# Linear attention on one core: Q transposed as pairs of bf16 in 4-byte elements, and zero-padded K features for the first two pairs

## The chip, the core and the metric

The kernel runs on one core of a Trainium2 chip. A core has five engines that run side by side, each with its own instruction queue: TensorE (PE, matrix products and transposes, results in PSUM), VectorE (DVE), ScalarE (ACT), GpSimd (POOL) and SyncE (SP). In this kernel POOL and SP issue the transfers between the device memory (HBM) and the core's own memory (SBUF, 128 partitions). The transfers run on 16 DMA engines. A group of weights is loaded into PE by a separate instruction (LDWEIGHTS, shown as PEld) ahead of the matmul that uses it.

The metric is the device time of one execution in microseconds (us). Before the change the median of three runs is 126.3 us (126.06 to 126.33).

## The reference

Q, K and V have 8 batches, 12 heads, 512 rows and 64 columns each, in float32. With the features `max(0, x) + 1` of Q and K:

```python
Q_feat = np.maximum(0, Q) + 1
K_feat = np.maximum(0, K) + 1
KV = np.einsum('bhkd,bhkv->bhdv', K_feat, V)
K_sum = np.sum(K_feat, axis=2)
numerator = np.einsum('bhqd,bhdv->bhqv', Q_feat, KV)
denominator = np.einsum('bhqd,bhd->bhq', Q_feat, K_sum)
return (numerator / (denominator[:, :, :, None] + 1e-10)).astype(np.float32)
```

There are 96 heads (batch times head). Each needs a 64x64 product KV over its 512 rows, a sum over K's features, and then a product of its Q features with both, and a division by row.

## The kernel before, in words

**Tiling.** The rows of all heads are taken as one list. A *group* g is eight heads, and there are 12 groups; two groups, 2s and 2s+1, are a *pair* s, and there are six pairs. On loading, one partition holds 32 successive rows, so 16 partitions hold one head, and 128 partitions hold eight heads. Pair 0 is loaded in half loads (`load_first_q`, `load_rest_q`, `load`), the other five pairs each in one load of V, one of K and one of Q (`load_pair`), all issued by POOL and turned from float32 into bf16 on the way; only the first half of Q comes through SP, as float32, into an output buffer. For pairs 1 to 5 these loads read 2 MB of HBM each and write 1 MB of SBUF.

**K and V.** `k_features` makes K's features on DVE (line 154, through `feature`). Since the partitions hold eight heads, V must be kept apart by head: `v_blocks` writes V four times, each time multiplied by a column of a mask that is 1 on the partitions of one head in each half of the partitions and 0 elsewhere (tile `v_all`, 68 columns per block, one of them the mask itself, which yields K_sum). DVE writes blocks 0 and 1 whole and one half of block 2 (line 171), ACT the other half of block 2 and block 3 whole (line 173). `keys_values` (line 195) then multiplies 64 partitions of K's features, 64 columns as weights, with 64 partitions of V's four blocks, 272 columns. The half h of the partitions goes to PSUM tile h. In groups 0 and 1 the result is on the output partitions of that group's half, so two of these matmuls lie on different parts of the PE array; from group 2 on the output half changes with each matmul, so four do. There are 64 such matmuls per group. `keys_values_copies` (line 209) copies the sums to `kva_all` on ACT, as 64x64 blocks on a diagonal with a 65th column for K_sum, for two heads at a time.

**Q.** `q_features` (line 154 as well) makes Q's features in bf16, with two rows of 64 features beside each other, so that 128 columns go through one transpose. `transposes` (line 222) turns 128x128 pieces on PE, 16 per group, into two PSUM tiles of eight; `transpose_copies` (line 227) copies each tile to `qt` on ACT. `out_matmuls` (line 237) takes 64 columns of `qt` as weights and `kva` as the moving operand, eight matmuls to a PSUM tile; `norms` (lines 253 and 254, DVE) divides by the last column and writes the float32 output tile. Both sets of PSUM tiles have two buffers each.

**Order.** The order on each engine is that in which the code is written (`manual_schedule`). After pair 0, `iteration(s)` runs for s = 1 to 5: it forms KV for the groups of pair s and, woven in between, the output of the groups of pair s - 1. On DVE an iteration does: the four norms of group 2s-2, Q's features of both groups of the pair, K's features and V's blocks of group 2s+1, the four norms of group 2s-1, and K's features and V's blocks of the next pair's first group. On ACT: V's blocks of 2s+1, the four copies of transposes, V's blocks of 2s+2, the four KV copies. On PE: output cells of group 2s-2 with the quarters of `keys_values` for group 2s between them, the transposes of both groups, output cells and `keys_values` for group 2s+1.

**Loads and stores.** V, K and Q have two input buffers each. `load_pair(s + 2)` stands behind `iteration(s)` on POOL, so its V load waits until DVE and ACT have read the last of V of pair s (lines 111 for V and K, 124 for Q). All stores but the last two groups' go through POOL as well (line 138); the first six stand behind the last load. The stores of the last two groups go through SP, in pieces (lines 143 to 151). Until its first output, DVE's work is the mask (line 330, which waits for the identity matrix that POOL makes) and the mask columns of `v_all` (lines 338 and 339).

Of the kernel before, what the change touches and what calls it, by code (L numbers as in the profile page):

```python
# [8 lines left out]
FP32 = mybir.dt.float32  # L9
# [10 lines left out]
def kernel(  # L20
# [36 lines left out]
    o_dram = view(out, C)  # L57

    const = ctx.enter_context(tc.tile_pool(name="const", bufs=1))
    in_pool = ctx.enter_context(tc.tile_pool(name="in_pool", bufs=IN_BUFS))  # L60
    kf_pool = ctx.enter_context(tc.tile_pool(name="kf_pool", bufs=2))
    qf_pool = ctx.enter_context(tc.tile_pool(name="qf_pool", bufs=3))
    mid_pool = ctx.enter_context(tc.tile_pool(name="mid", bufs=2))
    out_pool = ctx.enter_context(tc.tile_pool(name="out_pool", bufs=OUT_BUFS))
    recip_pool = ctx.enter_context(tc.tile_pool(name="recip", bufs=4))
    psum_kva = ctx.enter_context(tc.tile_pool(name="psum_kva", bufs=2, space=bass.MemoryType.PSUM))
    psum = ctx.enter_context(tc.tile_pool(name="psum", bufs=2, space=bass.MemoryType.PSUM))
    psum_qt = ctx.enter_context(tc.tile_pool(name="psum_qt", bufs=2, space=bass.MemoryType.PSUM))

    identity = const.tile([P, P], BF16, name="identity")  # L70
    NV = 4
    v_all = const.tile([P, 2, 2, C2, 4, DV], BF16, name="v_all")

    mask_row = const.tile([P, 396], FP32, name="mask")
# [7 lines left out]
    kfs = {}  # L82
    qfs = {}
    qts = {}
    outs = {}
# [71 lines left out]

    def k_features(g):
        k_raw = raw.pop(("k", g))
        kf = kf_pool.tile([P, C2, 2, D], BF16, name="kf")  # L160
        for n in range(2):
            feature(kf[:, :, n], k_raw[:, n])
        kfs[g] = kf

    def v_blocks(g, engine):
        v_raw = raw["v", g]
        for b in range(4):
            block = v_all[:, g % 2, :, :, b, 0:D]
            cut = 2 if b < 2 else 1 if b == 2 else 0
            if engine == "dve" and cut > 0:  # L170
                nc.vector.tensor_scalar_mul(block[:, 0:cut], v_raw[:, 0:cut], mask[:, b : b + 1])  # L171
            if engine == "act" and cut < 2:
                nc.scalar.mul(out=block[:, cut:], in_=v_raw[:, cut:], mul=mask[:, b : b + 1])  # L173

    def q_features(g):
        q_raw = raw.pop(("q", g))
        qf = qf_pool.tile([P, R, C // 2, 2, D], BF16, name="qf")
        for n in range(2):
            feature(qf[:, :, :, n], q_raw[n])
        qfs[g] = qf  # L180

    def keys_values(g, lo=0, hi=C2):
        kf = kfs[g]
        if g % 2 == 0 and lo == 0:
            kva_ps[g // 2] = [psum_kva.tile([P, BANK], FP32, name="kva_ps") for _ in range(2)]
        halves = kva_ps[g // 2]
        for c in range(lo, hi):
            for n in range(2):
                if g < 2:
                    eight, first, last_c = g, (c, n) == (0, 0), (c, n) == (C2 - 1, 1)  # L190
                else:
                    eight, first, last_c = n, g % 2 == 0 and c == 0, g % 2 == 1 and c == C2 - 1
                for h in range(2):
                    ps = slice(64 * h, 64 * h + 64)
                    nc.tensor.matmul(  # L195
                        halves[h][64 * eight : 64 * eight + 64, 0 : 4 * DV],
                        lhsT=kf[ps, c, n, :],
                        rhs=v_all[ps, g % 2, n, c],
                        start=first,
                        stop=last_c,  # L200
                    )

    def keys_values_copies(s):
        halves = kva_ps[s]
        for h in range(2):
            kva = kva_diag[(2 * s + h) % NV]
            for n in range(2):
                ps = slice(64 * n, 64 * n + 64)
                nc.scalar.copy(  # L209
                    out=kva[ps, :, n, :],  # L210
                    in_=halves[h][ps, 0 : 4 * DV].rearrange("p (b x) -> p b x", b=4)[:, :, 0:D1],
                )

    def transposes(g):
        qf = qfs.pop(g)
        if g % 2 == 0:
            qts[g // 2] = mid_pool.tile([P, C, P, R], BF16, name="qt")
        qt_ps[g] = [psum_qt.tile([P, 2, R, P], BF16, name="qt_ps") for _ in range(2)]
        for half in range(2):
            for c in range(2):  # L220
                for r in range(R):
                    nc.tensor.transpose(qt_ps[g][half][:, c, r], qf[:, r, 2 * half + c, :, :], identity)  # L222

    def transpose_copies(g):
        for half, t in enumerate(qt_ps.pop(g)):
            lo = g % 2 * 4 + 2 * half
            nc.scalar.copy(out=qts[g // 2][:, lo : lo + 2], in_=t.rearrange("p c r q -> p c q r"))  # L227

    def out_matmuls(g, h, i):
        qt = qts[g // 2]  # L230
# [2 lines left out]
        for c in range(4 * i, 4 * i + 4):  # L233
            for j in range(2):
# [87 lines left out]
    with tc.manual_schedule():  # L322
# [76 lines left out]
```

## Time and profile before

| | |
|---|---|
| median of three runs | 126.3 us (126.06 to 126.33) |
| the profiled execution | 126.47 us |
| its span, first to last instruction | 124.7 us |
| PE busy | 72.2 us (58%), 1344 matmuls |
| DVE busy | 81.9 us (66%), 185 instructions |
| ACT busy | 68.4 us (55%), 73 instructions |
| POOL busy | 24.8 us (20%) |
| HBM read and written | 37.75 MB and 12.58 MB, 404 GB/s over the span |

How to read it: the page divides the span into 40 equal slices of 3.1 us, with the busy share of each engine in tenths and, for the DMA engines, the mean busy share of all 16. The *granted clock* (PEclk) is the share of TensorE's full clock that the throttle let through. A group of instructions is given as line, engine, operation, tiles and shapes, count, then busy time and mean nanoseconds of one, then the idle time of the engine just before them and what ended most of it. Instructions of one engine overlap in the records: of matmuls that follow each other the start-to-start time is shorter than the duration of one. A DMA share slightly above 1 means that packets overlapped.

### The profile page before, as it was taken

How to read it: one execution, taken by the hardware profiler on the slowest of the kernel's cores; microseconds unless marked ns; L12 is line 12 of the kernel's file. 1: busy time of each engine (PE TensorE's matmuls, PEld its weight loads, DVE VectorE, ACT ScalarE, POOL GpSimd, SP SyncE). 2: the span in 40 equal slices, each digit the busy share in tenths (PEclk: the TensorE clock that was granted, in tenths of full speed). 3: DMA queues.
4: the chain of work that ended last, by engine and by line, in shares of the span. 5: the costliest groups of instructions: out<-in, count | busy, mean ns of one | idle time of the engine just before them, and what ended most of it. 6: DMA issues, size and time to landing. Idle time of an engine off the chain costs nothing.

```text
span 124.7 us, 3086 instructions
## 1 busy us (share of the span) xinstructions
PE 72.2 (58%) x1344; PEld 54.4 (44%) x1344; DVE 81.9 (66%) x185; ACT 68.4 (55%) x73; POOL 24.8 (20%) x52
## 2 busy tenths in 40 slices
PE   0000199692397949976796927979429995550000
PEld 0000299591266725754465714567216774320000
DVE  0475643006679997999979979798997945990000
ACT  0005827928955999199947998059990196000000
POOL 6990001500000600033000890220210202000000
PEclk9999999999859995899769995599975799955555
DMA  3999999999999999999999999999999999999991
GB/s 74 344 216 217 214 212 210 214 214 222 210 212 210 218 222 212 212 212 214 221 214 213 212 216 216 218 213 210 214 350 422 413 417 413 413 413 418 411 388 64
DMA packets 8902, 32.18 MB, mean 258 GB/s; under 512 B 568, under 2 KB 824, under 8 KB 8760
## 3 DMA queue, kind: packets, MB, share of 16 engines
q0 software_dynamic: 7520, 28.84, 93.9%
q1 hardware_dynamic: 1368, 3.15, 6.8%
q8 instruction: 10, 0.16, 0.5%
q14 instruction: 4, 0.03, 0.1%
HBM read 37.75 MB, written 12.58 MB: 404 GB/s over the span
## 4 chain that ended last, share of the span: by engine, by line
PE 32%; DMA 21%; ACT 18%; DVE 14%; issue 3%; POOL 1%; ACTq 0%; POOLq 0%
PE kva_ps L195 21%; DMA k_raw<-in_K_dram 14%; ACT qt L227 9%; PE o_ps L237 7%; DMA v_raw<-in_V_dram 7%; ACT v_all L173 6%; DVE o_sb L254 6%; DVE v_all L171 4%; PE qt_ps L222 4%; ACT kva_all L209 2%; DVE kf L154 2%; DVE recip L253 1%; ACT L173 1%; POOL v_raw L111 1%; POOL k_raw L114 1%
## 5 line engine op out<-in xcount | busy, mean ns | idle before, releaser
L195 PE MATMUL kva_ps<-v_all,kf 64*64 64x272 bf16 x768 | 41.0, 330 | 19.9 <-ACT v_all L173 18.3
L195 PEld LDWEIGHTS <-kf 64*64 64x64 bf16 x768 | 28.3, 125 | 25.7 <-DVE v_all L171 16.4
L173 ACT ACTIVATE v_all<-v_raw,mask 128x1024 bf16<-128x1024 bf16 (+1 forms) x24 | 36.5, 1578 | 3.1 <-DMA v_raw<-in_V_dram 3.0
L254 DVE TENSOR_TENSOR o_sb<-o_ps,recip 128x512 f32<-128x512 f32 x48 | 33.2, 691 | 1.7
L227 ACT COPY qt<-qt_ps 128x1024 bf16<-128x1024 bf16 x24 | 22.7, 1024 | 19.6 <-PE qt_ps L222 19.6
L237 PE MATMUL o_ps<-kva_all,qt 128*64 128x130 bf16 x384 | 21.4, 253 | 14.1 <-ACT kva_all L209 9.2
L237 PEld LDWEIGHTS <-qt 128*64 128x64 bf16 x384 | 14.9, 126 | 23.8 <-issue 9.6
L171 DVE TENSOR_SCALAR v_all<-v_raw,mask 128x2048 bf16<-128x2048 bf16 (+1 forms) x36 | 22.0, 665 | 3.2 <-DMA v_raw<-in_V_dram 3.2
L154 DVE TENSOR_SCALAR kf<-k_raw 128x1024 bf16<-128x1024 bf16 x24 | 9.4, 434 | 12.0 <-DMA k_raw<-in_K_dram 12.0
L222 PE MATMUL qt_ps<-identity,qf 128*128 128x128 bf16 x192 | 13.7, 219 | 4.9 <-ACT qt L227 4.8
L253 DVE RECIPROCAL recip<-o_ps 128x8 f32<-128x8 f32 x48 | 9.6, 201 | 8.3 <-PE o_ps L237 8.2
L111 POOL DMA_DIRECT2D v_raw<-in_V_dram x5 | 3.7, 730 | 53.5 <-ACT qt L227 23.7
L222 PEld LDWEIGHTS <-qf 128*128 128x128 bf16 x192 | 11.2, 97 | 7.0 <-issue 6.4
L138 POOL DMA_DIRECT2D out_dram<-o_sb x10 | 8.1, 819 | 25.5 <-DVE o_sb L254 13.7
L209 ACT CAST kva_all<-kva_ps 64x260 bf16<-64x260 f32 x24 | 9.0, 374 | 3.8 <-PE kva_ps L195 3.5
L154 DVE TENSOR_SCALAR qf<-q_raw 128x1024 bf16<-128x1024 bf16 x22 | 8.2, 430 | 0.1
L173 ACT ACT_TABLE_LOAD x1 | 1.3, 1283 | 10.7 <-DMA v_raw<-in_V_dram 10.7
L124 POOL DMA_DIRECT2D q_raw<-in_Q_dram x5 | 3.6, 722 | 0.0
L111 POOL DMA_DIRECT2D k_raw<-in_K_dram x5 | 3.6, 719 | 0.0
L330 DVE TENSOR_REDUCE mask<-identity 128x4 f32<-128x128 bf16 x1 | 0.3, 285 | 4.7 <-POOL identity masks.py:199 4.7
L344 POOL MEMSET kva_all<- 128x130 bf16 x16 | 2.4, 204 | 0.0
L339 DVE CAST v_all<-mask 128x128 bf16<-128x128 f32 x2 | 2.2, 1644 | 0.0
(11 smaller groups left out, 6.0 us busy)
## 6 DMA issues: line engine op xcount, KB each, us to landing
out_dram<-o_sb POOLq DMA_DIRECT2D x10, 1024.0 KB, 24.6
v_raw<-in_V_dram POOLq DMA_DIRECT2D x5, 1024.0 KB, 13.5
k_raw<-in_K_dram POOLq DMA_DIRECT2D x5, 1024.0 KB, 17.7
q_raw<-in_Q_dram POOLq DMA_DIRECT2D x5, 1024.0 KB, 21.9
o_sb<-in_Q_dram SPq DMA_DIRECT2D x1, 1024.0 KB, 5.0
k_raw<-in_K_dram POOLq DMA_DIRECT2D x2, 512.0 KB, 9.7
v_raw<-in_V_dram POOLq DMA_DIRECT2D x2, 512.0 KB, 11.6
out_dram<-o_sb SPq DMA_DIRECT2D x1, 1024.0 KB, 11.5
```

Of the source, the lines that this page charges most:

```text
L111: nc.gpsimd.dma_start(out=t, in_=drams[x][:, 2 * s : 2 * s + 2])
L138: nc.gpsimd.dma_start(out=o_to[:, g % 2 : 2 * NP : 2], in_=outs[s][:, g % 2 : 2 * NP : 2], single_packet=True)
L154: nc.vector.tensor_scalar(out=dst, in0=src, scalar1=1.0, scalar2=1.0, op0=ALU.add, op1=ALU.max)
L171: nc.vector.tensor_scalar_mul(block[:, 0:cut], v_raw[:, 0:cut], mask[:, b : b + 1])
L173: nc.scalar.mul(out=block[:, cut:], in_=v_raw[:, cut:], mul=mask[:, b : b + 1])
L195: nc.tensor.matmul(halves[h][64 * eight : 64 * eight + 64, 0 : 4 * DV], lhsT=kf[ps, c, n, :], rhs=v_all[ps, g % 2, n, c], start=first, sto ...
L209: nc.scalar.copy(out=kva[ps, :, n, :], in_=halves[h][ps, 0 : 4 * DV].rearrange("p (b x) -> p b x", b=4)[:, :, 0:D1],)
L222: nc.tensor.transpose(qt_ps[g][half][:, c, r], qf[:, r, 2 * half + c, :, :], identity)
L227: nc.scalar.copy(out=qts[g // 2][:, lo : lo + 2], in_=t.rearrange("p c r q -> p c q r"))
L237: nc.tensor.matmul(o_ps[64 * j : 64 * j + 64, c // 2 % 2, (c % 2) * W : (c % 2) * W + W], lhsT=qt[:, c, q : q + 16, :], rhs=kva[:, b], sta ...
L253: nc.vector.reciprocal(out=recip, in_=cells[:, :, :, :, D:D1])
L254: nc.vector.tensor_tensor(out=outs[g // 2][:, 2 * h + g % 2 : 2 * NP : NP, 4 * i : 4 * i + 4].rearrange("p n (b c) d -> p b c n d", b=2), ...
```

## The change

The change has five parts.

1. Q's features are written so that the elements of two rows alternate (`qf` gets a last dimension of 2). Two bf16 are then taken as one 4-byte element (`bitcast(FP32)`) and turned with a float32 identity: eight transposes of 128x128 4-byte elements per group in place of sixteen of bf16. The copies to `qt` move 512 4-byte elements per partition in place of 1024 bf16. `out_matmuls` reads every second bf16 of `qt` as weights. `qf` has two buffers in place of three.
2. For groups 0 to 3 (`WIDE = 2` pairs), K's features of the lower and the upper 64 partitions go to different columns of a tile twice as wide, whose other columns are zero on those partitions. One matmul then takes all 128 partitions and 128 weight columns: 32 matmuls per group in place of 64. `keys_values_copies` reads the sums from where they now lie. Groups 4 to 11 keep the four-part form.
3. The tiles for K's features are no longer taken from a pool in turn, but are two fixed ones; their zero columns are set at the start, by four instructions on DVE.
4. Block 2 of V is written wholly by ACT; DVE's half of it is gone.
5. The mask's row is 48 elements in place of 396, and `recip_pool` stands earlier.

```diff
-    qf_pool = ctx.enter_context(tc.tile_pool(name="qf_pool", bufs=3))
+    qf_pool = ctx.enter_context(tc.tile_pool(name="qf_pool", bufs=2))
...
-    identity = const.tile([P, P], BF16, name="identity")
+    identity = const.tile([P, P], FP32, name="identity")
...
+    WIDE = 2
+    kf_all = [wide.tile([P, C2, 2, 2, D], BF16, name=f"kf_all_{i}") for i in range(2)]
...
     def k_features(g):
         k_raw = raw.pop(("k", g))
-        kf = kf_pool.tile([P, C2, 2, D], BF16, name="kf")
+        kf = kf_all[g % 2]
         for n in range(2):
-            feature(kf[:, :, n], k_raw[:, n])
-        kfs[g] = kf
+            if g // 2 < WIDE:
+                for h in range(2):
+                    ps = slice(64 * h, 64 * h + 64)
+                    feature(kf[ps, :, n, h], k_raw[ps, n])
+            else:
+                feature(kf[:, :, n, 0], k_raw[:, n])
...
-            cut = 2 if b < 2 else 1 if b == 2 else 0
+            cut = 2 if b < 2 else 0
...
-        qf = qf_pool.tile([P, R, C // 2, 2, D], BF16, name="qf")
+        qf = qf_pool.tile([P, R, C // 4, 2, D, 2], BF16, name="qf")
         for n in range(2):
-            feature(qf[:, :, :, n], q_raw[n])
+            feature(
+                qf[:, :, :, n].rearrange("p r c d x -> p r c x d"),
+                q_raw[n].rearrange("p r (c x) d -> p r c x d", x=2),
+            )
...
+                if g // 2 < WIDE:
+                    nc.tensor.matmul(
+                        halves[eight][:, 0 : 4 * DV],
+                        lhsT=kf[:, c, n],
+                        rhs=v_all[:, g % 2, n, c],
+                        start=first,
+                        stop=last_c,
+                    )
+                    continue
...
     def transposes(g):
-        qf = qfs.pop(g)
+        qf = qfs.pop(g).rearrange("p r c n d x -> p r c (n d x)").bitcast(FP32)
         if g % 2 == 0:
-            qts[g // 2] = mid_pool.tile([P, C, P, R], BF16, name="qt")
-        qt_ps[g] = [psum_qt.tile([P, 2, R, P], BF16, name="qt_ps") for _ in range(2)]
+            qts[g // 2] = mid_pool.tile([P, C // 2, P, R, 2], BF16, name="qt")
+        qt_ps[g] = [psum_qt.tile([P, R, P], FP32, name="qt_ps") for _ in range(2)]
         for half in range(2):
-            for c in range(2):
-                for r in range(R):
-                    nc.tensor.transpose(qt_ps[g][half][:, c, r], qf[:, r, 2 * half + c, :, :], identity)
+            for r in range(R):
+                nc.tensor.transpose(qt_ps[g][half][:, r], qf[:, r, half], identity)
 
     def transpose_copies(g):
+        to = qts[g // 2].rearrange("p c q r x -> p c (q r x)").bitcast(FP32)
         for half, t in enumerate(qt_ps.pop(g)):
-            lo = g % 2 * 4 + 2 * half
-            nc.scalar.copy(out=qts[g // 2][:, lo : lo + 2], in_=t.rearrange("p c r q -> p c q r"))
+            nc.scalar.copy(
+                out=to[:, g % 2 * 2 + half].rearrange("p (q r) -> p q r", r=R),
+                in_=t.rearrange("p r q -> p q r"),
+            )
...
-                    lhsT=qt[:, c, q : q + 16, :],
+                    lhsT=qt[:, c // 2, q : q + 16, :, c % 2],
...
+        for t in kf_all:
+            for h in range(2):
+                zeros = t[64 - 64 * h : P - 64 * h].rearrange("p c n h d -> p (c n) h d")[:, :, h]
+                nc.vector.memset(zeros.bitcast(FP32), 0.0)
```

In the built program each of the 4-byte transposes is one instruction on PE, without a separate load of weights; all other matmuls keep theirs. The order of the work on each engine is otherwise that of before.

More of the change, by code (lines that the diff above doesn't have):

```diff
@@ L59 @@
     const = ctx.enter_context(tc.tile_pool(name="const", bufs=1))
+    recip_pool = ctx.enter_context(tc.tile_pool(name="recip", bufs=4))
+    wide = ctx.enter_context(tc.tile_pool(name="wide", bufs=1))
     in_pool = ctx.enter_context(tc.tile_pool(name="in_pool", bufs=IN_BUFS))
-    kf_pool = ctx.enter_context(tc.tile_pool(name="kf_pool", bufs=2))
-    qf_pool = ctx.enter_context(tc.tile_pool(name="qf_pool", bufs=3))
+    qf_pool = ctx.enter_context(tc.tile_pool(name="qf_pool", bufs=2))
     mid_pool = ctx.enter_context(tc.tile_pool(name="mid", bufs=2))
     out_pool = ctx.enter_context(tc.tile_pool(name="out_pool", bufs=OUT_BUFS))
-    recip_pool = ctx.enter_context(tc.tile_pool(name="recip", bufs=4))
     psum_kva = ctx.enter_context(tc.tile_pool(name="psum_kva", bufs=2, space=bass.MemoryType.PSUM))
@@ L68 @@
     psum_qt = ctx.enter_context(tc.tile_pool(name="psum_qt", bufs=2, space=bass.MemoryType.PSUM))
-    identity = const.tile([P, P], BF16, name="identity")
+    identity = const.tile([P, P], FP32, name="identity")
     NV = 4
     v_all = const.tile([P, 2, 2, C2, 4, DV], BF16, name="v_all")
-    mask_row = const.tile([P, 396], FP32, name="mask")
+    mask_row = const.tile([P, 48], FP32, name="mask")
     mask = mask_row[:, 0:4]
@@ L81 @@
     bufs = {}
-    kfs = {}
     qfs = {}
@@ L176, in q_features @@
         q_raw = raw.pop(("q", g))
-        qf = qf_pool.tile([P, R, C // 2, 2, D], BF16, name="qf")
+        qf = qf_pool.tile([P, R, C // 4, 2, D, 2], BF16, name="qf")
         for n in range(2):
-            feature(qf[:, :, :, n], q_raw[n])
+            feature(
+                qf[:, :, :, n].rearrange("p r c d x -> p r c x d"),
+                q_raw[n].rearrange("p r (c x) d -> p r c x d", x=2),
+            )
         qfs[g] = qf
     def keys_values(g, lo=0, hi=C2):
-        kf = kfs[g]
+        kf = kf_all[g % 2]
         if g % 2 == 0 and lo == 0:
@@ L196, in keys_values @@
                         halves[h][64 * eight : 64 * eight + 64, 0 : 4 * DV],
-                        lhsT=kf[ps, c, n, :],
+                        lhsT=kf[ps, c, n, 0],
                         rhs=v_all[ps, g % 2, n, c],
@@ L208, in keys_values_copies @@
                 ps = slice(64 * n, 64 * n + 64)
+                tile_, at = (n, slice(64 * h, 64 * h + 64)) if s < WIDE else (h, ps)
                 nc.scalar.copy(
                     out=kva[ps, :, n, :],
-                    in_=halves[h][ps, 0 : 4 * DV].rearrange("p (b x) -> p b x", b=4)[:, :, 0:D1],
+                    in_=halves[tile_][at, 0 : 4 * DV].rearrange("p (b x) -> p b x", b=4)[:, :, 0:D1],
                 )
     def transposes(g):
-        qf = qfs.pop(g)
+        qf = qfs.pop(g).rearrange("p r c n d x -> p r c (n d x)").bitcast(FP32)
         if g % 2 == 0:
-            qts[g // 2] = mid_pool.tile([P, C, P, R], BF16, name="qt")
-        qt_ps[g] = [psum_qt.tile([P, 2, R, P], BF16, name="qt_ps") for _ in range(2)]
+            qts[g // 2] = mid_pool.tile([P, C // 2, P, R, 2], BF16, name="qt")
+        qt_ps[g] = [psum_qt.tile([P, R, P], FP32, name="qt_ps") for _ in range(2)]
         for half in range(2):
-            for c in range(2):
-                for r in range(R):
-                    nc.tensor.transpose(qt_ps[g][half][:, c, r], qf[:, r, 2 * half + c, :, :], identity)
+            for r in range(R):
+                nc.tensor.transpose(qt_ps[g][half][:, r], qf[:, r, half], identity)
     def transpose_copies(g):
+        to = qts[g // 2].rearrange("p c q r x -> p c (q r x)").bitcast(FP32)
         for half, t in enumerate(qt_ps.pop(g)):
-            lo = g % 2 * 4 + 2 * half
-            nc.scalar.copy(out=qts[g // 2][:, lo : lo + 2], in_=t.rearrange("p c r q -> p c q r"))
+            nc.scalar.copy(
+                out=to[:, g % 2 * 2 + half].rearrange("p (q r) -> p q r", r=R),
+                in_=t.rearrange("p r q -> p q r"),
+            )
     def out_matmuls(g, h, i):
```

## The prediction

> **What bounds the kernel now.** I read the page's 40 slices first, because they show every engine and the transfers side by side.
>
> ```profile
> DVE  0475643006679997999979979798997945990000
> PEclk9999999999859995899769995599975799955555
> DMA  3999999999999999999999999999999999999991
> ```
>
> The DMA row is the only one that is full from the second slice to the last but one; VectorE comes next, then PE and ACT, all with gaps. Then stretches of the trace (columns: window, its length, busy time of PE, PEld, DVE, ACT, POOL with counts, clock, DMA share, GB/s).
>
> ```profile
> 20.00:25.00 5.00, 4.04 (x65) 3.46 (x63) 0.00 (x0) 4.11 (x5) 2.14 (x3) 1.00 1.07 216
> 60.00:65.00 5.00, 4.80 (x96) 3.15 (x94) 4.17 (x11) 3.66 (x4) 0.00 (x0) 0.66 1.05 212
> 115.00:118.00 3.00, 0.00 (x0) 0.00 (x0) 0.00 (x0) 0.00 (x0) 0.00 (x0) 0.50 1.02 408
> 121.00:122.00 1.00, 0.00 (x0) 0.00 (x0) 0.00 (x0) 0.00 (x0) 0.00 (x0) 0.50 0.81 297
> 122.00:123.00 1.00, 0.00 (x0) 0.00 (x0) 0.00 (x0) 0.00 (x0) 0.00 (x0) 0.50 0.17 64
> ```
>
> From 4 to 121 us no stretch has a DMA share below 1.02: first loads, then stores, with never a hole. The page's 37.75 + 12.58 MB in 124.7 us is 404 GB/s over everything. The change leaves every byte of this, so computing can cost time only where it makes the queue run dry. How far is it from that? The timeline of POOL says when loads are issued, the issues say when the last load ahead of them lands (same-named Q load, issue to landing).
>
> ```profile
> 41.19 0.72 POOL L111 DMA_DIRECT2D v_raw<-in_V_dram  x1 [17.70 <-DVE recip L253]
> 55.14 0.72 POOL L111 DMA_DIRECT2D v_raw<-in_V_dram  x1 [11.80 <-ACT qt L227]
> 69.15 0.72 POOL L111 DMA_DIRECT2D v_raw<-in_V_dram  x1 [11.88 <-ACT qt L227]
> ```
>
> The Q load issued at 22.77 needs 25.6 us and lands at 48.4; those of 42.62 and 56.56 (20.5 and 21.2 us) land at 63.1 and 77.8. So the loads at 41.19, 55.14 and 69.15 are issued 7.2, 8.0 and 8.6 us ahead. Not all of that is slack: I estimate 1.5 us between the last byte and the landing (a pair's 6.29 MB land in 14.7 us, 428 GB/s; the first six half loads are 6.3 MB as well, are moving from about 1.8, so should be through at 16.5, yet the sixth lands at 18.0), and 1.5 us from issue to first byte (first issue 1.27, DMA full at 3). Usable slack: about **4.2, 5.0 and 5.6 us**. Landings are 14.7 us apart, iterations 14.0: the kernel computes a little faster than it is fed. In the last stage VectorE ends at 111.97 and the last store lands at 123.8; SP's last store is issued 4.8 us after VectorE's end (116.78), and a load of 192 KB or more needs some 2.4 us uncrowded, so VectorE could end about **4.6 us** later (123.8 - 7.2 = 116.6).
>
> **The change, part by part.** Sums are against the profiled execution, 126.47 us (span 124.7 and 1.8 around it), 0.17 above the median of 126.3.
>
> ```profile
> L222 PE MATMUL qt_ps<-identity,qf 128*128 128x128 bf16 x192 | 13.7, 219 | 4.9 <-ACT qt L227 4.8
> L222 PEld LDWEIGHTS <-qf 128*128 128x128 bf16 x192 | 11.2, 97 | 7.0 <-issue 6.4
> L154 DVE TENSOR_SCALAR qf<-o_sb 128x1024 bf16<-128x1024 f32 x2 | 1.4, 685 | 0.0
> L173 ACT ACTIVATE v_all<-v_raw,mask 128x1024 bf16<-128x1024 bf16 x12 | 13.9, 1158 | 3.1 <-DMA v_raw<-in_V_dram 3.0
> ```
>
> *Transposes.* 16 per iteration in place of 32. Eight now take 0.61 us, so they start (0.61 - 0.219) / 7 = 56 ns apart. No row has a 4-byte transpose. Low end 56 ns; high end four times that, 224 ns (and 4 x 97 = 388 ns if weight loads are not hidden either). I take the nearest row for one piece of 128x128 brought in alone, the 97 ns load, rounded to 0.11 us, since the separate load instructions go and a self-loading matmul may not hide them. The stretch of transposes then shrinks from 3.24 us (51.86 to 55.10, two waits for ACT in it) to about 2.1.
> The Trainium skill, TensorE: Matmul & The Clock Gate, sections Weight-path perf modes and LDWEIGHTS, says that the fast weight load is not for FP32 and that a load takes columns / 1.2 GHz, which is 107 ns by estimate and gives the same sum; its Terms call the transpose mode four times faster for FP32. FP8 and Floating Point Precision, TensorE Precision Notes, gives true FP32 four passes, which would be 224 ns and the first rival below; no run here shows which.
>
> *Their copies on ACT.* 512 f32 elements for 1024: between the 260-element row (374 ns) and 1024 (1018 ns) this is 0.59 us, saving 4 x 0.43 = 1.7 us per iteration. *V's third block* moves from DVE to ACT: two halves more per iteration, (1.998 - 1.158) x 2 = +1.7 us on ACT, which evens out; DVE loses 2 x 0.40 = 0.8 us.
>
> *Q's features* write every second element. Low end the present 0.335 us from start to start; high end one element at a time, from the 512-element f32 row of L254 (0.61 from start to start) 1.2 us. I take 0.60, the start-to-start time of the f32-source row above, the nearest: 4 x 0.27 = +1.1 us per iteration.
> The skill's VectorE: DVE Perf Modes, Mode 2x_1P, wants step 1 for packed pairs and so would leave half rate here, not a quarter: the same choice.
>
> DVE per iteration: about 13.1 busy + 1.1 - 0.8 = 13.4; with the present 0.7 of waits for PE 14.1, under 14.7. ACT's chain from first transpose to the first kva copy, 7.2 us now (51.86 to 59.09), becomes 0.5 + 4 x 0.55 + 3.9 = 6.6. Steady iterations therefore still keep up.
>
> *K on all partitions, first two pairs.* Each group's features become four instructions of the same length: +0.67 us DVE. 64 matmuls become 32. In groups 0 and 1 two ran at once (64 in 3.89 us), so 32 at 0.121 us cost the same. In groups 2 and 3 four ran at once (32 in 1.12): 32 full ones cost 3.9 to 6.3 us (at the 0.196 us of the first group) against 3.4 and 2.4. This is the cost that is not hidden in its own iteration. On the way to the load of 41.19: ACT's V block +0.9 to 1.5, first quarter +0.4, second quarter at a low clock +0.8, Q +1.1, K +0.7, V -0.4: **3.4 to 4.0 us** against 4.2 of slack. The next iteration starts 3 to 5 us late (slack 5.0); later iterations give part back, being up to 0.6 us faster than the feed. VectorE ends at about 112 to 115, before 116.6.
>
> In groups 0 and 1 the same V blocks let PE start 0.85 us later (15.07 now) and the loads of 21.35 go out at 22.2, when 11 us are still queued (33.5). Nothing.
>
> *Output matmuls* load every second element of qt as weights. The count of columns, 64, is the same and the load is hidden at 0.42 us for eight (row L237: 126 ns for one, several at once); low end nothing, high end 0.06 us each if a strided load takes twice as long and cannot hide, 64 x 0.06 = 3.8 us of PE per iteration, which would act as rival 1 does. I take nothing, the row's column count being unchanged. The copies of KV read another half of the partitions, 64 x 260 as before. Nothing.
>
> *Zeroing* on DVE: 384 elements take 0.38 us, so 4 x 1024 take about 4.1 us; DVE is idle until 4.72 (it waits for the identity). Were they twice as long, mask and v_all come 4 us later, V's first blocks at about 12 instead of 10.63, still before ACT's 15.03 that lets the first matmul go. Nothing. The wider identity on POOL (0.26 + 0.29) delays loads issued at 7.01 that start moving near 17. Two Q buffers instead of three: each was read an iteration earlier. Nothing.
>
> Sum: 126.47 - 0.17 + 0 = **126.3 us**.
>
> **Rivals.**
> *1. A 4-byte transpose costs four times as much (slower).* At 224 ns the stretch is 3.8 us, ACT's copies end when they do now and V's longer blocks add 0.95 per iteration: 14.95, more than the feed of 14.7. With 5 us late from group 2 and 3 and three such iterations VectorE ends near 119, 2.4 past its limit; 0.3 more for late loads: 129. At 388 ns 2.6 us more per iteration: 140 or more. It decides from about 0.17 to 0.2 us per transpose. For it: twice the bytes per element, and the strided weights of the output matmuls would push the same way; against it: 56 ns is one column per element now, and the column count of a transpose stays 128.
> *2. The load of 41.19 comes just too late (slower).* The 3.4 to 4.0 against 4.2 is close. If K's halves cost 0.42 instead of 0.335 and the quarters run at the low clock, 4.5 to 5: a hole of 0.3 to 1.5 us, 127.1. The clock row (dips to 5 to 7) speaks for it.
> *3. Q's features at one element at a time (slower).* +3.4 - 0.8 on DVE: 16.4 us per iteration, 1.7 over the feed: about 133.
> *4. The end gets tidier (faster).* After 121 us the share falls to 0.81, 0.17, 0.04: about 1 us that stores issued sooner could close, if iterations without DMA waits end earlier: 125.5. Against it: the stores wait in a full queue anyway.
>
> **How the numbers follow.** 0.2% (0.25 us) is about what can be told from no change here. Forecast 0.44 (own range 125.8 to 126.8; within 0.25 us 0.27, faster 0.11, slower 0.06); rival 1 0.20, rival 2 0.20, rival 3 0.06, rival 4 0.05, several small delays 0.05. Faster 0.16, same 0.27, slower 0.57. The range from 125.8 to 131 leaves out the dearer half of rival 1 (0.08), rival 3 (0.06) and a few of rival 4.
>
> **What would show it.** Right: DMA share above 1 from 4 to 121, the third V load issued by about 45, transposes near 0.11 us apart, copies of qt near 0.59, qf near 0.6 to 0.7, VectorE ending before 116. Wrong: a slice of DMA below 9 near 46, 61 or 75; transposes over 0.17 us apart; V loads more than 14.7 us apart; VectorE's last norm after 117.

## The result, and the profile after

The changed kernel takes 127.94 us (median of 22 executions, 126.17 to 130.66); the kernel before, run beside it, takes 126.38 us (median of 22, 126.02 to 126.55). The ratio is 1.0057, with a 95% interval of 1.004 to 1.0074: slower, where the prediction took no change as likeliest. This ratio, like all ratios below, leaves out executions more than 1.5% above the fastest of their kernel (here 10 of 22, and 7 of 12 in a second set, whose ratio is 1.0005 [0.9977, 1.0033]), so it is smaller than that of the medians (1.012, and 1.013 in the second set). So the loss is not the same in every execution, and the spread is part of the result: 0.5 us before, 4.5 us after.

The profiled execution of the changed kernel took 127.04 us (span 125.3), 0.57 more than the one of before (126.47, span 124.7). Its page has these rows for the granted clock and the transfers, in 40 slices of 3.13 us:

```profile
PEclk9999999999679999999999999999955999655555
DMA  3999999999999999999999999999999999999991
GB/s 102 320 211 216 215 215 212 212 218 216 211 213 217 216 211 179 209 212 220 212 214 215 213 217 213 216 215 213 214 341 419 420 408 415 417 413 417 415 390 44
```

The DMA row is as full as before and shows nothing. The row below it does: in the sixteenth slice, 47.0 to 50.1 us, 179 GB/s moved where its neighbours have 209 to 216. Stretches of 1 us around it, and at the end (window, its length, busy time and count of PE, PEld, DVE, ACT, POOL, clock, DMA share, GB/s):

```profile
46.00:47.00 1.00, 1.00 (x15) 0.81 (x15) 0.57 (x3) 0.30 (x1) 0.19 (x1) 1.00 1.39 201
47.00:48.00 1.00, 1.00 (x11) 0.85 (x9) 1.00 (x4) 0.00 (x0) 0.00 (x0) 1.00 0.75 152
...
122.00:123.00 1.00, 0.00 (x0) 0.00 (x0) 0.00 (x0) 0.00 (x0) 0.00 (x0) 0.50 0.44 162
```

From 46 to 47 the share is above its usual 1.06 while fewer bytes move: for its bytes a packet took about 1.4 times as long, and the time in which it waits counts as busy. Then the share falls. The rows of 45 to 50 us, before and after:

```profile
45.00:50.00 5.00, 3.91 (x68) 2.52 (x72) 4.19 (x10) 4.82 (x7) 0.00 (x0) 0.73 1.04 210
```

```profile
45.00:50.00 5.00, 4.20 (x53) 3.02 (x57) 4.26 (x11) 2.90 (x6) 1.19 (x2) 1.00 1.06 190
```

That is 190 GB/s against 210 before, 20 x 5 = 100 KB too little, about 0.5 us of a queue that moves 213. All that follows is late by 0.6 to 0.9 us: the third V load lands at 53.9 instead of 53.3, the last Q load at 93.3 instead of 92.5, and the last stores slide into 122 to 123 (162 GB/s; it was 64). VectorE ends no later than before (its last instruction ends at 111.80, before at 112.05), so the stores at the end are not what is late.

The hole lies at the seam between two sets of loads. The timeline of POOL has V's loads:

```profile
44.03 0.72 POOL L114 DMA_DIRECT2D v_raw<-in_V_dram  x1 [19.62 <-issue]
...
58.10 0.72 POOL L114 DMA_DIRECT2D v_raw<-in_V_dram  x1 [11.91 <-ACT qt L247]
...
71.32 0.72 POOL L114 DMA_DIRECT2D v_raw<-in_V_dram  x1 [11.07 <-ACT qt L247]
```

The first of them was issued at 41.19 before and is 2.84 us later; the Q load ahead of it lands at 48.3, before at 48.4. What made it late is in the timelines of PE and of DVE, one fence each. Before:

```profile
33.09 0.66 PE L195 MATMUL kva_ps<-v_all,kf 64*64 64x272 bf16 x16 [3.21 <-ACT v_all L173]
...
34.26 1.12 PE L195 MATMUL kva_ps<-v_all,kf 64*64 64x272 bf16 x16
```

```profile
36.84 1.42 DVE L154 TENSOR_SCALAR qf<-q_raw 128x1024 bf16<-128x1024 bf16 x4
38.18 0.75 DVE L154 TENSOR_SCALAR kf<-k_raw 128x1024 bf16<-128x1024 bf16 x2
38.85 1.80 DVE L171 TENSOR_SCALAR v_all<-v_raw,mask 128x2048 bf16<-128x2048 bf16 x3
```

After:

```profile
32.64 1.97 PE L204 MATMUL kva_ps<-v_all,kf_all 128*128 128x272 bf16 x8 [4.06 <-ACT v_all L180]
...
35.12 1.47 PE L204 MATMUL kva_ps<-v_all,kf_all 128*128 128x272 bf16 x8
```

```profile
37.83 2.62 DVE L157 TENSOR_SCALAR qf<-q_raw 128x1024 bf16<-128x1024 bf16 x4
40.34 1.73 DVE L157 TENSOR_SCALAR kf_all<-k_raw 64x1024 bf16<-64x1024 bf16 x4
42.08 1.42 DVE L178 TENSOR_SCALAR v_all<-v_raw,mask 128x2048 bf16<-128x2048 bf16 x2
```

The first two quarters of the second pair's full matmuls take 1.97 and 1.47 us (before 0.66 and 1.12), at a granted clock of 0.50 and 0.73. VectorE waits for the output cells between them, and then Q's and K's features take 1.2 and 1.0 us more, V's blocks 0.4 less. The other pieces of the change came out near their prices. These are the groups of the page that answer to those shown of before:

```profile
L247 ACT COPY qt<-qt_ps 128x512 f32<-128x512 f32 x24 | 12.9, 589 | 16.8 <-PE qt_ps L242 16.7
...
L242 PE MATMUL qt_ps<-identity,qf 128*128 128x128 f32 x96 | 13.3, 281 | 3.9 <-DVE qf L157 2.4
...
L157 DVE TENSOR_SCALAR qf<-q_raw 128x1024 bf16<-128x1024 bf16 x22 | 14.6, 741 | 0.4 <-DMA q_raw<-in_Q_dram 0.4
```

Eight transposes in a row take 1.09 us, so they start (1.09 - 0.281) / 7 = 0.116 us apart. The program has no separate load of weights for them, but the profile shows a load beside each (L242 PEld, 96 of 140 ns); whether that load sets the 0.116 us, no run shows.

### The profile page after: what moved, and what is told of

Its sections match the earlier page's. It is cut to its first block, busy times and chain, and to the rows that moved or that the text cites. A ratio compares the mean times of both kernels' runs of the same rounds, so it can differ in the third digit from the quotient of the medians.

```text
span 125.3 us, 2642 instructions
## 1 busy us (share of the span) xinstructions
PE 69.8 (56%) x1120; PEld 51.0 (41%) x1120; DVE 89.4 (71%) x185; ACT 69.0 (55%) x73; POOL 26.7 (21%) x52
## 4 chain that ended last, share of the span: by engine, by line
DVE 32%; DMA 25%; PE 17%; ACT 10%; issue 2%; POOL 2%; ACTq 0%; POOLq 0%
DVE o_sb L277 13%; DMA k_raw<-in_K_dram 13%; DMA v_raw<-in_V_dram 12%; PE kva_ps L204 9%; DVE qf L157 7%; ACT v_all L180 6%; DVE v_all L178 5%; PE o_ps L260 4%; DVE kf_all L157 3%; PE qt_ps L242 3%; DVE recip L276 3%; PE kva_ps L214 2%; ACT qt L247 2%; ACT kva_all L229 2%; POOL k_raw L117 1%
## 5 line engine op out<-in xcount | busy, mean ns | idle before, releaser
L180 ACT ACTIVATE v_all<-v_raw,mask 128x2048 bf16<-128x2048 bf16 x24 | 46.6, 1995 | 2.3 <-DMA v_raw<-in_V_dram 2.1
L204 PE MATMUL kva_ps<-v_all,kf_all 128*128 128x272 bf16 x128 | 18.8, 307 | 21.7 <-ACT v_all L180 20.0
L214 PE MATMUL kva_ps<-v_all,kf_all 64*64 64x272 bf16 x512 | 21.4, 298 | 4.6 <-DVE v_all L178 4.6
L204 PEld LDWEIGHTS <-kf_all 128*128 128x128 bf16 x128 | 13.3, 106 | 25.7 <-DVE v_all L178 15.0
L247 ACT COPY qt<-qt_ps 128x512 f32<-128x512 f32 x24 | 12.9, 589 | 16.8 <-PE qt_ps L242 16.7
L157 DVE TENSOR_SCALAR kf_all<-k_raw 64x1024 bf16<-64x1024 bf16 (+1 forms) x32 | 13.2, 433 | 10.7 <-DMA k_raw<-in_K_dram 10.4
L178 DVE TENSOR_SCALAR v_all<-v_raw,mask 128x2048 bf16<-128x2048 bf16 x24 | 17.4, 767 | 1.1 <-DMA v_raw<-in_V_dram 1.0
L214 PEld LDWEIGHTS <-kf_all 64*64 64x64 bf16 x512 | 13.9, 113 | 8.1 <-issue 3.3
L242 PE MATMUL qt_ps<-identity,qf 128*128 128x128 f32 x96 | 13.3, 281 | 3.9 <-DVE qf L157 2.4
L242 PEld LDWEIGHTS qt_ps<-identity,qf 128*128 128x128 f32 x96 | 10.2, 140 | 6.2 <-DVE qf L157 2.9
```

The lines of the kernel that those rows point to most:

```text
L157: nc.vector.tensor_scalar(out=dst, in0=src, scalar1=1.0, scalar2=1.0, op0=ALU.add, op1=ALU.max)
L204: nc.tensor.matmul(halves[eight][:, 0 : 4 * DV], lhsT=kf[:, c, n], rhs=v_all[:, g % 2, n, c], start=first, stop=last_c,)
L214: nc.tensor.matmul(halves[h][64 * eight : 64 * eight + 64, 0 : 4 * DV], lhsT=kf[ps, c, n, 0], rhs=v_all[ps, g % 2, n, c], start=first, sto ...
L242: nc.tensor.transpose(qt_ps[g][half][:, r], qf[:, r, half], identity)
L247: nc.scalar.copy(out=to[:, g % 2 * 2 + half].rearrange("p (q r) -> p q r", r=R), in_=t.rearrange("p r q -> p q r"),)
```

## The experiments

Two theories stood at first. A: the third V load is issued too late for the seam, and only that costs time. B: lateness of this size does no harm by itself; something in the changed kernel's own work on VectorE holds the transfers up. The kernel before, run beside each set, had a median of 126.36 to 126.45 us.

### Which part of the change

Three kernels take the change apart. In two of them fewer pairs have full matmuls; nothing else differs from the changed kernel:

```diff
-    WIDE = 2
+    WIDE = 0      # the other kernel: 1
```

> Everything of the change but the matmuls over all 128 partitions: groups 0 to 3 go back to the four-part matmuls (the tiles stay double wide, the zeroing stays). Theory (the third pair's V load, issued at 44.03 instead of 41.19, comes too late and the DMA queue runs dry once, near 47 us; the full matmuls of groups 2 and 3 and the doubled K instructions are what makes it late): that load goes out at 41 to 42, no window from 4 to 121 us has a DMA share below 0.9, 126.2 to 126.5 us, and the runs lie within 0.6 us of each other as those of before do. Rival (the 4-byte transposes, the strided Q features and the V block on ACT are to blame): 0.5 to 0.7 us slower than before, load at 43 or later. Rival (it is the end: stores of the last groups): the load is early, but the last slice and the time stay as after the change, 127.

> The change with the full matmuls in groups 0 and 1 only. Theory: groups 0 and 1 cost nothing (32 of 0.121 us for 64 of 0.0605), the price lies in groups 2 and 3 alone, where four matmuls ran at once: load at 41 to 42.5, no hole, 126.2 to 126.5 us. Rival (both pairs share the price): half of the loss stays, about 126.7.

The third has the full matmuls of both pairs and everything that belongs to them (padded K, zeroing, rows of the KV copies), but Q's features, transposes, copies and the split of V's blocks of before.

> Only the full-partition matmuls of groups 0 to 3 with their doubled K instructions and the zeroing; Q's path, the transposes and the split of V are those of before. Theory: the load goes out at about 43.7 (Q's features 1.2 us shorter than after the change, V's third block 0.4 longer, ACT's V blocks about 0.5 later), so at the edge: 126.3 to 126.9 us, and with more spread than before. Rival (the Q path is to blame): as before, 126.3, load at 41 to 42.

Measured:

| kernel | us, median (range) | ratio, 95% | third V load issued |
|---|---|---|---|
| no full matmuls, the rest of the change | 126.62 (126.27 to 126.66) | 1.0018 [1.0008, 1.0027] | 42.18 |
| full matmuls in the first pair alone, the rest | 126.42 (126.18 to 126.73) | 1.0006 [0.9997, 1.0015] | 42.67 |
| full matmuls in both pairs alone | 126.29 (126.04 to 126.81) | 0.9999 [0.9988, 1.0010] | 44.02 |
| the whole change | 127.94 (126.17 to 130.66) | 1.0057 [1.0040, 1.0074] | 44.03 |

The first two loads go out a little later than expected (41 to 42, and 41 to 42.5), and the first kernel's time is 0.1 us above its range. No part alone costs what the whole costs, and without the second pair's full matmuls the spread is gone as well. The surprise is the third row: its load is issued at the same time as in the changed kernel, but no hole follows. Its row of 45 to 50 us has 215 GB/s, where the changed kernel has 190:

```profile
45.00:50.00 5.00, 4.18 (x53) 3.02 (x56) 4.51 (x12) 4.12 (x7) 1.16 (x2) 1.00 1.07 215
```

Either 44.0 is just the edge, or theory B is right. The next two sets ask that.

### How late may the load be

In the kernel before, POOL writes zeros into the load's own buffer first, and nothing else in the program is changed. Three lengths make a ladder:

```diff
         if len(groups) == 2:
+            if x == "v" and s == 3:
+                nc.gpsimd.memset(t[:, :, 0:24], 0.0)      # 3072 elements; once, or twice,
+                nc.gpsimd.memset(t[:, 0, 0:20], 0.0)      # or once with this one of 1280
             nc.gpsimd.dma_start(out=t, in_=drams[x][:, 2 * s : 2 * s + 2])
```

> The kernel before, with one GpSimd memset of 3072 elements per partition in front of the third V load, so that this load is issued later (by some 2 to 3 us: 43.2 to 44.2 instead of 41.19) while nothing else is changed. Theory A (the usable slack of this load was over-estimated: the first software load of the program, issued at 1.26, shows its first bytes only near 4.6 to 5.0, so 3.4 to 3.8 us and not 1.5 are needed ahead of the seam): no loss up to an issue near 43.2, then about 1 us per us, so 126.3 to 127.0. Theory B (lateness alone does no harm before 45.4, as the slack of 4.2 us says, and what costs time in the changed kernel is its own work on VectorE, which holds up the making of the load's descriptors): 126.3 to 126.4 and no hole at 46 to 50.

> The same with two such memsets: the third V load is issued some 4 to 6 us later, at 45.2 to 47.2. Theory A: a hole of 1.5 to 4 us from about 46.7 on, 127.8 to 130.5. Theory B with the slack of 4.2 us: a hole of 0 to 1.8 us, 126.3 to 128.1. In both the hole ends at issue plus the time to the first bytes, which this run measures: 3.4 to 3.8 us by A, 1.5 by the estimate of the prediction.

> The kernel before with one memset more than in the run of one memset (1280 elements beside 3072): the third V load is issued at about 44.9. A, by the two runs of the ladder (43.69 lost nothing, 46.12 lost 2.0 us of time): the loss begins at about 44.0, so 0.7 to 1.0 us here, 127.0 to 127.5. If the queue loses in jumps and not us for us: 126.3 to 126.5, or 128 and more.

The row of 45 to 50 us, for one memset, then for one and the short one, then for two:

```profile
45.00:50.00 5.00, 3.58 (x64) 2.34 (x64) 4.37 (x10) 4.93 (x7) 0.91 (x2) 0.78 1.05 209
```

```profile
45.00:50.00 5.00, 3.29 (x56) 1.98 (x56) 4.78 (x10) 4.74 (x7) 2.06 (x3) 0.72 1.06 192
```

```profile
45.00:50.00 5.00, 1.80 (x40) 1.29 (x40) 4.93 (x9) 4.10 (x5) 2.97 (x4) 0.92 0.85 141
```

| third V load issued | us, median (range) | above the kernel before |
|---|---|---|
| 43.69 | 126.36 (126.23 to 126.52) | nothing (ratio 0.9997 [0.9988, 1.0006]) |
| 44.91 | 127.03 (126.84 to 127.25) | 0.62 (126.41) |
| 46.12 | 128.44 (128.13 to 129.82) | 2.03 (126.41) |

So lateness alone does cost time, with none of the changed kernel's work about: from the second step to the third, 1.21 us of lateness cost 1.41 us by the medians. By the rows of 45 to 50 us the hole itself is about 0.4 and 1.6 us. (The profile of the last kernel is of its longest execution, 129.82 us; the issue at 46.12 is taken to be that of the others too. And the ladder is not quite pure: while the second memset of 2.66 us runs, VectorE's two K features take 2.81 us in place of 0.75. VectorE still ends at 114.1, before the prediction's limit of 116.6.) Going back from 44.91 at that slope, or at 1 us per us, the loss begins at 44.3 to 44.4, about 4 us ahead of the previous Q load's landing (48.3). Both longer delays came out as theory A expected (127.0 to 127.5 and 127.8 to 130.5). Its edge of 43.2, in the first expectation, was 1 us too early, and theory B with a slack of 4.2 us is wrong: by it nothing is lost at 44.91.

The time from issue to bytes can be read in the last kernel, in half microseconds (issue at 46.12):

```profile
46.50:47.00 0.50, 0.00 (x0) 0.00 (x0) 0.50 (x1) 0.50 (x1) 0.50 (x2) 1.00 0.48 90
47.00:47.50 0.50, 0.00 (x0) 0.00 (x0) 0.50 (x2) 0.50 (x2) 0.50 (x1) 1.00 0.21 41
47.50:48.00 0.50, 0.00 (x0) 0.00 (x0) 0.50 (x2) 0.50 (x1) 0.50 (x2) 1.00 1.75 172
48.00:48.50 0.50, 0.00 (x0) 0.00 (x0) 0.50 (x3) 0.50 (x1) 0.27 (x1) 1.00 0.34 41
...
49.50:50.00 0.50, 0.50 (x8) 0.40 (x8) 0.50 (x1) 0.00 (x0) 0.00 (x0) 0.50 1.00 197
```

The queue thins out from 46.5, 1.8 us ahead of the landing. The new load's packets begin between 47.5 and 48.0, about 1.5 us after the issue, which is what the prediction estimated. But they begin slowly: the next half microsecond moves 41 GB/s, and 197 are reached only from 49.5 on, over 3 us after the issue. The first expectation's figure of 3.4 to 3.8 us was read off wrongly: at the program's start the packets of the software queue begin at 5.03, but SP's own load passes through the same engines until 5.34, so they may have been waiting behind it.

### The changed kernel once more

> The changed kernel once more, for a second profile of it. Times of 126.2 to 130.7, median about 127.9, as before. If the issue of the third V load decides the time (A), this profile's hole at the seam is longer or shorter than the first one's by as much as the load is issued later or earlier than 44.03, and its time follows; if the delay lies behind the issue (B), the load stands at about 44.0 again and the hole differs all the same.

Median 128.08 us (125.78 to 131.40). The profiled execution was one of the longest, 131.04 us. Its timelines of PE and POOL and two stretches:

```profile
33.54 1.97 PE L204 MATMUL kva_ps<-v_all,kf_all 128*128 128x272 bf16 x8 [4.06 <-ACT v_all L180]
...
36.02 1.99 PE L204 MATMUL kva_ps<-v_all,kf_all 128*128 128x272 bf16 x8
```

```profile
45.67 0.72 POOL L114 DMA_DIRECT2D v_raw<-in_V_dram  x1 [21.37 <-issue]
...
61.28 0.72 POOL L114 DMA_DIRECT2D v_raw<-in_V_dram  x1 [13.45 <-ACT qt L247]
```

```profile
45.00:50.00 5.00, 4.81 (x37) 3.02 (x37) 2.99 (x9) 2.94 (x2) 2.15 (x3) 0.66 0.95 165
...
63.00:64.00 1.00, 1.00 (x32) 0.79 (x33) 0.97 (x3) 1.00 (x1) 0.43 (x1) 1.00 0.88 82
```

Here the load went out at 45.67, 1.64 us later than in the first profile, and the hole is longer: 165 GB/s against 190. That is theory A, though the hole grows by 0.6 us only (25 x 5 = 125 KB). Set beside the ladder, it is the first profile that stands out: at 45.67 the ladder's steps (0.4 us at 44.91, 1.6 at 46.12) give a hole of about 1.2 us and 1.06 is found, at 44.03 they give none and 0.5 is found. The second profile also shows where the spread comes from. The first quarter starts 0.9 us later, and the second quarter runs at a granted clock of 0.50 through its whole length (1.99 us against 1.47 at 0.73). The lateness does not heal: group 3's quarters, too, ran slowly (1.93 us for the first), and the next V load came 15.6 us after this one, more than the 14.7 us of feed. It is only 3.4 us ahead of the previous Q load's landing (64.7), and a second hole follows at 63 to 64. It sheds light on the third kernel of the table above as well: there the same two quarters took 1.97 and 1.99 us, so its 44.02 is reached with both quarters at the low clock, while the changed kernel's 44.03 has the second partly at the full clock; with both at the low clock that kernel's load is at 45.67.

### The clock

If the half clock in these quarters is what makes the load late, keeping PE busy in the idle 4.06 us ahead of them must heal the change:

```diff
             out_matmuls(*cells[k])
+            if g == 0 and k == 1:
+                spare = psum_qt.tile([P, R, P], FP32, name="qt_ps")
+                for _ in range(16):
+                    nc.tensor.matmul(
+                        spare[0:D1].rearrange("p r q -> p (r q)"),
+                        lhsT=kva_diag[0][:, 0, 0, :],
+                        rhs=qts[0][:, 0].rearrange("p q r x -> p (q r x)")[:, 0 : R * P],
+                        start=True, stop=True,
+                    )
```

> The changed kernel with 16 matmuls more, of 65x512, on operands that lie ready and into a spare PSUM tile that nobody reads, put where PE otherwise stands idle from 28.6 to 32.6. They change no result; they only keep PE busy. Theory A (the third V load comes late because the full matmuls of the second pair run at half the granted clock after that idle stretch, 1.97 and 1.47 to 1.99 us for a quarter): both quarters take about 1.1 us, the load is issued 1.2 to 1.8 us earlier, at 42.3 to 43.3, no hole, 126.2 to 126.6 with a spread under 1 us. Theory D (the clock has no part in it, VectorE and ScalarE alone set the issue): the load stays at 44.0 or later and the time at 127 to 128.5, spread as before.

The timeline of PE:

```profile
28.70 3.64 PE L298 MATMUL qt_ps<-qt,kva_all 128*65 128x512 bf16 x16
32.83 1.09 PE L204 MATMUL kva_ps<-v_all,kf_all 128*128 128x272 bf16 x8 [0.49 <-DVE o_sb L277]
...
34.20 1.10 PE L204 MATMUL kva_ps<-v_all,kf_all 128*128 128x272 bf16 x8
```

126.43 us (125.98 to 126.61), ratio 0.9996 [0.9987, 1.0005]: 16 matmuls that compute nothing bring the time back to that of the kernel before, and the spread from 4.5 to 0.6 us. Both quarters take 1.1 us. Theory D falls. The row of the granted clock, which dips to 6 and 7 in the first profile, stands at 9 through these slices. The load is issued at 42.76, and no hole follows (213 GB/s from 45 to 50 us).

The Trainium skill, TensorE: Matmul & The Clock Gate (The HAM clock gate), says that PE falls to half rate after an idle window of about 3.4 us, and that the windows run freely, so that the count of slow matmuls differs from run to run. The traces agree: 4.06 us of idle time ahead of quarters of 1.97 us, 0.49 us ahead of quarters of 1.09 us, and two profiles of the same kernel with 1.47 and 1.99 us for the same quarter. They do not agree on the 3.4 us throughout: in the third kernel of the table above PE went idle at 29.4 us, for 3.21 us, and the granted clock is 0.50 already from 30.9 on; and in the second profile of the changed kernel group 3's first quarter ran slowly (granted clock 0.52) after 1.66 us of idle time. What counts as idle for such a window is not shown here.

### Q's path and V's split

Two more kernels show what the remaining parts add to the lateness. One is the changed kernel with V's third block split between VectorE and ScalarE again (`cut = 2 if b < 2 else 1 if b == 2 else 0`); the other has the full matmuls and V's third block on ScalarE, but Q's path of before.

> The whole change, but with V's third block split between VectorE and ScalarE as before. Theory A: VectorE's chain to the third V load has 0.4 to 0.8 us more in it, so the load is issued at 44.4 to 45 and the hole is as long as that of the changed kernel or longer: 127.8 to 129. Theory C (ScalarE's longer V blocks, 1.95 us each, running from 42.4 to 46.3 right over the issue, are what slows the load's start): no hole, 126.3 to 126.6.

> The full matmuls and V's third block on ScalarE, but Q's features, transposes and copies as before. A: without Q's 1.0 us the load is issued 0 to 0.9 us later than in the run of the full matmuls alone (44.02, at the edge): 44.0 to 44.9, 126.3 to 127.2, a spread between theirs (0.8 us) and that of the changed kernel (4.5 us). If Q's path itself (and not its length) is what costs: 126.3 with a spread under 0.8.

The first: 127.39 us (126.32 to 129.60), ratio 1.0063 [1.0038, 1.0087], by the ratio no better than the whole change, by the median 0.6 us better and below the 127.8 to 129 expected; with 1.0 us lost, theory C falls. The expected 44.4 to 45 for the load did not show, because the profile caught the fastest execution (126.32 us, load at 43.38, no hole). The second: 126.54 us (126.27 to 127.25), ratio 1.0019 [1.0004, 1.0034], load at 43.94. So the full matmuls alone bring the load to the edge and lose nothing, V's block moves it a little over in some executions, and Q's features, 1.2 us longer and ahead of the load in VectorE's order, push it over in most. So it takes the second pair's full matmuls and Q's features together; V's block adds a little.

### K and V ahead of Q on VectorE

The lateness can be taken away by order as well: in each iteration K's features and V's blocks of the second group, which the load waits for, before Q's features.

```diff
-        q_features(a)
-        q_features(b)
         if not end:
             k_features(b)
             v_blocks(b, "dve")
+        q_features(a)
+        q_features(b)
```

> The whole change, but in each iteration VectorE makes the K features and V blocks of the pair's second group ahead of Q's features, so that the V load no longer waits for the 2.5 us of Q's features; the transposes get their input 3 us later. Theory (the late V load is all the loss): load at 41 to 42, no hole, 126.2 to 126.6 us with the small spread of before, although the computing gets no shorter and may end later. Rival (the computing as such, or the end, sets the time): 127 or more, since PE gets its transposes later. Rival (the transfers themselves are slower with the new addresses or the zeroing): 127, no hole.

129.64 us (128.65 to 132.14), ratio 1.0224 [1.0191, 1.0257]: worse than the change itself, though the load's instruction begins at 41.55 and, as the theory expected, no hole follows at this seam (214 GB/s from 45 to 50 us). The timeline of all engines there:

```profile
40.93 2.60 DVE L157 TENSOR_SCALAR qf<-q_raw 128x1024 bf16<-128x1024 bf16 x4
41.55 2.13 POOL L114 DMA_DIRECT2D v_raw<-in_V_dram  x1 [17.24 <-issue]
```

The instruction takes 2.13 us instead of 0.72 and ends at 43.68, 0.15 us after the last of Q's features. It does so at 58.09 and 73.61 again, and these two loads end only 3.1 and 4.0 us ahead of the previous landings (63.3 and 79.8). Two later holes go with them: 195 GB/s from 60 to 65 us and 175 from 75 to 80, where the kernel before has 212 and 214. They are about 0.4 and 0.9 us of the 2.4 by which the profiled execution (128.76 us) is longer. To tell this from the strided writes, the same order was given to the kernel before, whose Q features write contiguously.

> The kernel before with the one reordering of the run that put K's features and V's blocks ahead of Q's: VectorE writes Q's features, here with contiguous writes of 0.335 us each, while GpSimd issues the third V load (near 39.8, with the features running to about 40.6). In that run the load's instruction took 2.13 us in place of 0.72 and ended 0.26 us after the last of Q's features (2.60 us for four). If any bf16 feature on VectorE holds the instruction up, it takes 1.0 to 1.1 us here; if only those with strided writes do, 0.72. Either way the load goes out 5 us ahead of the seam, so no hole: 126.2 to 126.6.

The same stretch of its timeline:

```profile
39.25 1.42 DVE L154 TENSOR_SCALAR qf<-q_raw 128x1024 bf16<-128x1024 bf16 x4
39.87 0.96 POOL L111 DMA_DIRECT2D v_raw<-in_V_dram  x1 [16.39 <-DVE v_all L171]
```

0.96 us, again 0.15 us past the end of the features, in all three of these loads (the 0.26 of the expectation counts from the start of the norm behind them): contiguous features hold the instruction up as well, for as long as they last. The time was a miss: 127.04 us (126.45 to 128.37), ratio 1.005 [1.0013, 1.0087], without a hole at the seam (212 GB/s from 45 to 50). The order costs time by itself in the profiled execution, one of the long ones (128.32 us): VectorE's last norm starts at 120.28, where it starts at 111.36 in the order of before, and the DMA row falls to 6 in one of the last slices of stores. In the first of these two kernels the last norm is as late (120.41). So of its loss some 1.3 us are in the two later holes, none at the first seam, and the rest goes with the late end; this pair of runs does not test the third V load's share of the change.

## Why the prediction was wrong

**What bounds the kernel** held: the transfers are the bound, and time was lost only where their queue ran thin. The ladder shows this without any of the change. ("No share below 1.02" holds for the long stretches it read; by single microseconds the kernel before goes down to 0.97, from 49 to 50.)

**The slack of the third V load** is the step that failed. The prediction put the load 7.2 us ahead of the previous Q load's landing and took 1.5 us off at either end, which left 4.2. The runs give about 3.1 (41.19 to some 44.3). The 1.5 us between the last byte and the landing were nearly right (the queue thins 1.8 us ahead of it), and the 1.5 us from issue to first byte can be seen in the trace of the longest delay. What was left out is that the load is slow for another 1 to 2 us after its first bytes. The evidence taken for the 1.5 (first issue 1.27, DMA full at 3) was also not evidence for it: until 5.0 us only SP's queue moves, and the software queue's packets begin at 5.03. So 4.1 us go off the 7.2, not 3.0: 1.8, 1.5 and the slow start.

**The lateness**, 3.4 to 4.0 us, was about right as a middle: the two profiles have 2.84 and 4.48. Set against a slack of 3.1 it would have given a hole of 0.3 to 0.9 us and so 126.6 to 127.2 by the prediction's own sum. Its terms, measured: ScalarE's V block, +0.9 to 1.5 predicted, +0.86 (the first quarter starts 3.95 us after ScalarE's first V block, before 3.09); second quarter +0.8, measured +0.35 and +0.87; Q +1.1, measured +1.20; K +0.7, +0.98; V -0.4, -0.38. Only the first quarter was mis-sized: +0.4 predicted, 0.66 to 1.97 us measured, +1.31. With PE kept busy it took 1.09, +0.43, so the 0.4 is its price at the full clock, and the other 0.9 is the clock, which the prediction counted for the second quarter alone. Not foreseen was that ScalarE starts on these blocks earlier than before (at 28.69 and 29.60 instead of 30.00), which takes 1.31 and 0.40 off. The sums, 3.0 and 4.4 us, account for the two profiles. The step was also treated as one number; the clock makes it a different one in each execution, which is where the spread comes from.

**The rivals.** Rival 2 is what happened, by the mechanism and under the conditions it named: K's halves cost 0.43 us (1.73 / 4) instead of 0.335, and the quarters ran at the low clock. That its 127.1 us is the first profile's 127.04 is luck: it set 4.5 to 5 us of lateness against 4.2 of slack, where this profile has 2.84 against some 3.1. The median, 127.94, is beyond it; in the second profile the hole is longer and comes again at the next seam. It had a chance of 0.20 against 0.44, from a slack counted 1 us too long. Rival 1 is out: transposes are 0.116 us apart, well below its 0.17 (0.11 taken, from the row of a 97 ns load; that the size came out does not show that reason). Rival 3 is out: Q's features are 0.63 us apart from start to start (0.60 taken, 1.2 at one element at a time). Rival 4 did not show.

**The other steps** held. Copies of qt took 589 ns (0.59 predicted), ScalarE's V blocks 1995 ns (1998 in the prediction's working); VectorE ended at 111.80, before 116.6; the zeroing was hidden. Later iterations did keep up in the first profile (V loads 14.1 and 13.2 us apart) and not in the second (15.6). In the list of what would show the prediction wrong, the sign was the wrong row: the DMA share of the slice stays at 9, since a packet that waits counts as busy, and the hole stands in GB/s alone.

**What stays open.** The full matmuls alone have their load at 44.02 without a hole, the changed kernel at 44.03 with one of about 0.5 us; by the ladder's edge of 44.3 neither should have one. So the hole of the first profile is not explained by its load's issue alone, and what tells the two apart was not tested; for that half microsecond a hold-up by the changed kernel's own work, theory B, is not excluded. The kernel with no full matmuls is 0.2 us slower than before (interval 0.1 to 0.3) with no hole at all; its cause is open.

## What to carry to other kernels

Where a queue of transfers is the bound, find the load that is issued least ahead of its turn, and measure how much later it may come, for instance by a ladder of delays in the unchanged kernel, before counting several added pieces of work as hidden; here the load had to go out 4.0 to 4.6 us ahead of the previous landing, not the 3.0 of the estimate. Read the bytes moved, not the share of busy time, to see whether a queue is fed. And price a matmul that follows an idle stretch at the low clock: the same matmuls took 1.1 us with PE kept busy ahead of them and 2.0 without.

## What the runs showed that was not expected

- GpSimd's instruction for a load, 0.72 us, is stretched by VectorE's bf16 features: to 2.13 us while four strided ones ran (2.60 us), to 0.96 us behind four contiguous ones (1.42 us), each time to 0.15 us after their end, and not by the norms from PSUM that ran beside it elsewhere (0.72 at 44.03). The Trainium skill, SBUF — State Buffer (the "DVE blocks DMA" trap), says that certain VectorE modes lock GpSimd out of a shared port until the operation ends, so that it cannot write its descriptors; the traces agree, with the addition that four operations in a row held it to the end of the last. That the port is the cause is argued, not shown. It goes the other way too: GpSimd's memset of 2.66 us in the ladder stretched two K features on VectorE from 0.75 to 2.81 us.
- 16 matmuls without use, 3.64 us of PE, make the changed kernel 1.2% faster by the medians (127.94 to 126.43).
- A bf16 write of every second element costs 0.63 us per 1024 elements where a contiguous one costs 0.335, and a 4-byte transpose of 128x128 0.116 us where a 2-byte one costs 0.056.
- No kernel tried is faster than the one before: those without a hole in the loads and without later stores all end within 0.3 us of it, at the pace of the transfers.
